# A transformer trunk on one core: one modulation row summed on VectorE in place of TensorE

## The chip, the cores and the metric

The kernel runs on one core of a Trainium2 chip. The time is the device time of one execution in microseconds (us), and the median of several runs is given. The core has five engines that run side by side: TensorE (PE in the profile; its weight loads are PEld), VectorE (DVE), ScalarE (ACT), GpSimd (POOL) and SyncE (SP), which here only issues DMA transfers. Engines wait for each other through semaphores, and each runs its own list of instructions in order.

## The reference, cut to what matters

There are two decoder layers over 512 tokens of width 1024, with 16 heads of 64. Each layer derives six rows of 1024 numbers (shift, scale and gate, once for attention and once for the feed-forward part) from the conditioning vector `c`:

```python
c_act = jax.nn.silu(c)
for i in range(DEPTH):
    mod = jnp.einsum('bd,dm->bm', c_act, w_mod[i]) + b_mod[i]
    sh_a, sc_a, gt_a, sh_f, sc_f, gt_f = jnp.split(mod, N_MOD, axis=-1)
    h = modulate(rmsnorm(x, g_mix_pre[i]), sh_a, sc_a)
    ...                                   # q, k, v; stick-breaking attention in layer 0
    x = x + gt_a[:, None, :] * rmsnorm(o, g_mix_post[i])
    h = modulate(rmsnorm(x, g_ffn_pre[i]), sh_f, sc_f)
    ...                                   # gated feed-forward part with a causal convolution of 3 taps
    x = x + gt_f[:, None, :] * rmsnorm(y, g_ffn_post[i])
```

`modulate(h, shift, scale)` is `h * (1 + scale) + shift`. One such row is a product of a vector of 1024 with a matrix of 1024 x 1024: 4 MB of weights are read once for few operations each. In layer 0 the attention weight of a key is its own sigmoid times the product of (1 - sigmoid) over the keys between it and the query.

## The kernel before, in words

**Staging.** A first stage (`begin`, to about 56 us) makes the shift and scale of layer 0's attention, the modulated input, and the first projections. Then `attention` runs layer 0's heads to about 220 us; the output projection, the feed-forward part and layer 1 follow.

**The loop over heads.** `attention` goes through h = 0 to 16, of which the last only finishes head 15. For each head it writes four blocks of scores, of 512, 384, 256 and 128 keys (`scores`: two matmuls into a PSUM bank `ps`). Of each block ScalarE makes two sigmoids (`bt` in SBUF, and `ps` in place), VectorE scans the second into running products (`om` for 512 and 384 keys, in place in `ps` for the short ones), and GpSimd (long blocks) or VectorE (short ones) multiplies `bt` by it (`stick`). The blocks of the head before are transposed (`pa` to `at`), and after each second head `weighted` multiplies them with the values into a bank `po`. All banks come from one pool of eight in turn, so a matmul into a new bank waits until the bank's last reader is done. TensorE's time between is filled with the projections of later heads (`pqk`, from weight tiles `wf` that ScalarE and GpSimd split into high and low parts `wh` and `wl`; three matmuls make one product), in portions that the table `UNITS` sets. `queries` and `keys` take a finished projection apart into `qa`, `qb`, `kh` and `kl`.

**Modulation rows beside the heads.** The three rows that layer 0 needs after its attention are made in steps, by generators in a `Background`, between the heads:

- `mod_part_pe` (lines 175 to 200) makes a row's columns on TensorE: for each half of 512 columns four loads of 512 KB (`wm`), then a group of 16 matmuls into a bank `pm` (line 191), a transpose of it on VectorE (`mf`, 194), and small copies and one reduction into the columns `mc`. It does the scale and the shift of the feed-forward part, SC_F and then SH_F: four groups.
- `mod_row` (202 to 230) sums the gate row GT_A on VectorE: for each of eight blocks of 128 rows two loads of 256 KB and two multiply-adds of 128x512 (`acc`, 223); then two transposes (`tr`), two reductions, and small steps; the gate line is written to memory (`gtd`) and broadcast back (`gb`), and multiplied by a gain into `gt` (249).

Each head's end steps the first background from head 1 and the second from head 2 on; odd heads step the first once more, ahead of `weighted`.

**What sets the order.** TensorE and SyncE run in the order in which the program is written; ScalarE, VectorE and GpSimd are ordered by a scheduler.

Of the kernel before, what the change touches and what calls it, by code (L numbers as in the profile page):

```python
# [8 lines left out]
F32 = mybir.dt.float32  # L9
# [6 lines left out]
P = 128  # L16
# [21 lines left out]
def trunk(ctx, tc, x, c, w_mod, b_mod, g_mix_pre, g_mix_post, w_qkv, w_o, w_fg, b_fg,  # L38
# [8 lines left out]
    def nm(s):  # L47
        serial[0] += 1
        return f"{s}_{serial[0]}"
# [4 lines left out]
    def slot(s, dt=F32R):  # L54
        return sb.tile([P, 512], dt, tag="slot", name=nm(s), bufs=NS)
# [17 lines left out]
    make_identity(nc, idn)  # L73
    onesf = cst.tile([P, P], F32, name="onesf")
    nc.vector.memset(onesf, 1.0)
    ones = cst.tile([P, P], F32R, name="ones")
    nc.vector.tensor_copy(ones, onesf)
    mhalf = cst.tile([P, 1], F32, name="mhalf")
    nc.vector.memset(mhalf, -0.5)
    mask = cst.tile([P, P], F32, name="mask")  # L80
# [16 lines left out]
    def b_col(l, comp):  # L97
        return colA[:, 48 * l + 8 * comp : 48 * l + 8 * comp + 8]

    def g_col(l, comp):  # L100
        o = (96 if comp == SC_A else 112) + 8 * l
        return colA[:, o : o + 8]
# [40 lines left out]
    def mod_part(l, comp):  # L143
        row = comp in (GT_A, GT_F)
        acc = sb.tile([P, D], F32, tag="acc", name=nm("acc"), bufs=1)
        lo_c = comp * D
        if row:
            nc.gpsimd.memset(acc, 0.0)
            nc.sync.dma_start(acc[0:1, :], b_mod[l : l + 1, lo_c : lo_c + D])
        for d in range(ND):  # L150
            w = t4("wm")
            nc.sync.dma_start(w, w_mod[l, d * P : (d + 1) * P, lo_c : lo_c + D])
            if d == 0 and not row:
                nc.vector.tensor_scalar(acc, w, csil[:, 0:1], None, op0=ALU.mult)
            else:
                nc.vector.scalar_tensor_tensor(acc, w, csil[:, d : d + 1], acc, op0=ALU.mult, op1=ALU.add)  # L156
            yield
        turned, part = t4("tr"), sb.tile([P, 32], F32, tag="part", name=nm("part"), bufs=1)
        nc.vector.transpose(turned, acc)
        nc.vector.tensor_reduce(part, turned.rearrange("p (b c) -> p b c", c=32), axis=AX.X, op=ALU.add)  # L160
        yield
        s = quadrants(part, 32, nc.gpsimd)
        if row:
            gp = t4("gp")
            yield from mod_line(l, comp, s, [gp[:, :512], gp[:, 512:]])
            return
        res = cst.tile([P, ND], F32, name=nm("mc"))
        columns_of(res, s, nc.gpsimd)
        yield
        nc.vector.tensor_tensor(res, res, b_col(l, comp), op=ALU.add)  # L170
        if comp in (SC_A, SC_F):
            nc.vector.scalar_tensor_tensor(res, res, 1.0, g_col(l, comp), op0=ALU.add, op1=ALU.mult)
        made[l, comp] = res

    def mod_part_pe(l, comp):

        res = cst.tile([P, ND], F32, name=nm("mc"))
        for h in range(2):
            c0 = comp * D + 512 * h
            w = []  # L180
            for i in range(4):
                if i == 2:
                    yield
                w.append(t4("wm") if i % 2 else sb.tile([P, D], F32, tag="xn", name=nm("wm"), bufs=2))
                nc.sync.dma_start(w[i].rearrange("p (d e) -> p d e", d=2),
                                  w_mod[l].rearrange("(d p) e -> p d e", p=P)[:, 2 * i : 2 * i + 2, c0 : c0 + 512])
            yield
            ps = bank("pm")
            for d in range(ND):
                q = 32 * (d % 4)  # L190
                nc.tensor.matmul(ps[q : q + 32, :], c32[:, d, :], w[d // 2][:, 512 * (d % 2) : 512 * (d % 2) + 512],
                                 start=d < 4, stop=d > 3, tile_position=(0, q))
            f = slot("mf", F32)
            nc.vector.transpose(f, ps)
            columns_of(res[:, 4 * h : 4 * h + 4], quadrants(f[:, ::32], 16, nc.vector), nc.vector)
            yield
        nc.vector.tensor_tensor(res, res, b_col(l, comp), op=ALU.add)
        if comp in (SC_A, SC_F):
            nc.vector.scalar_tensor_tensor(res, res, 1.0, g_col(l, comp), op0=ALU.add, op1=ALU.mult)
        made[l, comp] = res  # L200

    def mod_row(l, comp):

        lo_c = comp * D
        acc, part = [slot("acc", F32) for _ in range(2)], sb.tile([P, 32], F32, tag="part", name=nm("part"), bufs=1)

        def load(d):
            r = [slot("wm", F32) for _ in range(2)]
            for h in range(2):
                nc.sync.dma_start(r[h], w_mod[l, d * P : (d + 1) * P, lo_c + 512 * h : lo_c + 512 * h + 512])  # L210
            return r

        for h in range(2):
            nc.gpsimd.memset(acc[h], 0.0)
            nc.sync.dma_start(acc[h][0:1, :], b_mod[l : l + 1, lo_c + 512 * h : lo_c + 512 * h + 512])
        w = load(0)
        for d in range(ND):
            yield
            now = w
            if d < ND - 1:  # L220
                w = load(d + 1)
            for h in range(2):
                nc.vector.scalar_tensor_tensor(acc[h], now[h], csil[:, d : d + 1], acc[h], op0=ALU.mult, op1=ALU.add)
        yield
        for h in range(2):
            turned = slot("tr", F32)
            nc.vector.transpose(turned, acc[h])
            nc.vector.tensor_reduce(part[:, 16 * h : 16 * h + 16], turned.rearrange("p (b c) -> p b c", c=32), axis=AX.X, op=ALU.add)
        yield
        yield from mod_line(l, comp, quadrants(part, 32, nc.vector), [slot("gp", F32) for _ in range(2)])  # L230

    def mod_line(l, comp, s, gp):

        g = (g_mix_post if comp == GT_A else g_ffn_post)[l].rearrange("(o n) -> o n", o=1)
        for h in range(2):
            nc.sync.dma_start(gp[h], g[:, 512 * h : 512 * h + 512].to_broadcast([P, 512]))
        rows = sb.tile([32, 32], F32, tag="gtr", name=nm("gtr"), bufs=1)
        nc.vector.transpose(rows, s)
        yield True
        line = dr.tile([1, D], F32, name=nm("gtd"))  # L240
        nc.sync.dma_start(line.rearrange("o (b r) -> (o b) r", r=32), rows)
        yield True
        wide = t4("gb")
        nc.sync.dma_start(wide, line.to_broadcast([P, D]))
        yield True
        res = sb.tile([P, D], F32, tag="gt", name=nm("gt"), bufs=2)
        for h in range(2):
            cs = slice(512 * h, 512 * h + 512)
            nc.vector.tensor_tensor(res[:, cs], wide[:, cs], gp[h], op=ALU.mult)
        made[l, comp] = res  # L250
# [346 lines left out]
    def attention(l, qk, vt, ot, filler, units, bgs):  # L597


        get = cums_of.get(l)  # L600
        late, ats, cums = None, {}, {}
        for h in range(NH + 1):
            p, hd = divmod(h, 2)
            done = [0, 0]

            def fill(n=1):
                done[0] += n
                u = (units[h] * min(done[0], 12) + 11) // 12 - done[1]
                done[1] += u
                filler.run(u)  # L610

            if h < NH and hd == 0:
                ot.append((slot("oh"), slot("ol")))
            if get and h < NH:
                for i in range(h, min(h + 2, NH)):
                    if i not in cums:
                        cums[i] = get(i)
            probs = {}
            for qb in range(NT - 1, -1, -1):
                if h < NH:  # L620
                    ps, n = scores(l, hd, qb, qk[p, 0], qk[p, 1])
                    probs[qb] = stick(ps, n) if l % 2 == 0 else fox(ps, qb, cums[h])
                    fill(2)
                if late and qb == 2:
                    ats[late[1] % 2] = transposed(late[0])
            fill(2 if h < NH else 10)
            if h % 2:
                for bg in bgs[:1]:
                    bg.step()
            if late and hd == 0:  # L630
                weighted(p - 1, vt, ats, ot[p - 1])
                ats = {}
            fill(12)
            late = (probs, h)
            if h:
                for bg in bgs[: 1 + (h > 1)]:
                    bg.step()
# [196 lines left out]

    cums_of = {}
    for l in range(DEPTH):
        bgs = [Background([(l, SC_F), (l, SH_F)], mod_part_pe), Background([(l, GT_A)], mod_row)] if l == 0 else []
        scale = -0.125 if l % 2 else 0.125
        vt, qk, kl[:] = {}, {}, low_rooms()
        if l == 0:  # L840
# [173 lines left out]
```

## Time and profile before

| | |
|---|---|
| median of three runs | 1255.88 us (1254.57 to 1257.66) |
| the profiled execution | 1257.99 us, its span in the trace 1256.2 us |
| mean granted TensorE clock | 0.996 |
| busy: TensorE, VectorE, ScalarE, GpSimd | 98%, 56%, 47%, 23% of the span |

Times in the rows of the prediction are microseconds from the start of that span. "x16" behind a row means 16 instructions shown as one, and what stands in square brackets is how long the engine had been idle ahead of it, and for whom.

### The profile page before, as it was taken

The numbers are of one execution on the slowest core, as the hardware profiler recorded it, in microseconds if no ns is written. First come the engines' busy times: TensorE is split into PE (matmuls) and PEld (weight loads), VectorE is DVE, ScalarE is ACT, GpSimd is POOL, SyncE is SP. The second block draws the span as 40 slices with busy tenths as digits, with TensorE's granted clock in tenths as the row PEclk, the third lists the DMA queues.
The fourth block names the chain that finished last, engine by engine and source line by source line (L and its number), as shares of the span: only waits on it lengthen the run. The fifth ranks groups of instructions, "written<-read, shape, count | busy, mean of one in ns | idle before, by whom it ended". The sixth has DMA issues, their size and how long they took to land.

```text
span 1256.2 us, 16873 instructions
## 1 busy us (share of the span) xinstructions
PE 1234.3 (98%) x6300; PEld 1024.5 (82%) x6300; DVE 707.3 (56%) x1168; ACT 587.0 (47%) x1104; POOL 286.6 (23%) x348
## 2 busy tenths in 40 slices
PE   7999999999999999999999999999999999999997
PEld 5877877789888888888887888877988888888886
DVE  5667676277788988422364665564684444442233
ACT  7576666475333333222366565665733333331221
POOL 4775555510000000000216554452000000000000
PEclk9999999999999999999999999999999999999999
DMA  9737532225586677323405433333173333333231
GB/s 286 222 123 254 181 115 94 92 68 168 168 267 232 207 248 230 102 90 99 136 1 170 125 94 118 110 113 113 38 232 117 101 93 92 100 101 98 89 99 67
DMA packets 179400, 171.29 MB, mean 136 GB/s; under 512 B 7385, under 2 KB 152177, under 8 KB 179318
## 3 DMA queue, kind: packets, MB, share of 16 engines
q1 hardware_dynamic: 179142, 170.15, 43.6%
q8 instruction: 49, 0.80, 0.3%
q14 instruction: 33, 0.27, 0.1%
q10 hardware_dynamic: 176, 0.07, 0.0%
HBM read 168.01 MB, written 2.18 MB: 135 GB/s over the span
## 4 chain that ended last, share of the span: by engine, by line
PE 88%; DVE 4%; ACT 3%; issue 2%; DMA 1%; POOL 1%; SPq 0%; ACTq 0%; POOLq 0%; DVEq 0%
PE pgu L345 13%; PE pgu L346 13%; PE pgu L344 13%; PE pd L345 6%; PE pd L344 6%; PE pd L346 6%; PE pqk L344 4%; PE pqk L346 4%; PE pqk L345 4%; PE ps L466 3%; PE po L516 3%; PE pv L344 3%; PE pv L346 3%; PE pv L345 3%; PE pa L504 3%
## 5 line engine op out<-in xcount | busy, mean ns | idle before, releaser
L270 ACT CAST wh<-wf 128x1024 fp32r<-128x1024 f32 (+2 forms) x178 | 185.4, 1042 | 288.4 <-PE pgu L345 134.5
L345 PE MATMUL pgu<-htl,wh 128*128 128x512 f32 (+1 forms) x736 | 276.3, 375 | 0.6 <-DVE htl L406 0.6
L344 PE MATMUL pgu<-hth,wh 128*128 128x512 f32 (+1 forms) x736 | 276.4, 375 | 0.0
L346 PE MATMUL pgu<-hth,wl 128*128 128x512 f32 (+1 forms) x736 | 276.1, 375 | 0.0
L271 DVE TENSOR_TENSOR wl<-wf,wh 128x1024 fp32r<-128x1024 f32 x122 | 149.3, 1224 | 215.2 <-ACT wh L270 212.8
L345 PEld LDWEIGHTS pgu<-htl,wh 128*128 128x128 f32 x736 | 138.5, 188 | 26.1 <-DVE htl L406 1.0
L344 PEld LDWEIGHTS pgu<-hth,wh 128*128 128x128 f32 x736 | 138.5, 188 | 25.1
L346 PEld LDWEIGHTS pgu<-hth,wl 128*128 128x128 f32 x736 | 138.5, 188 | 24.6
L271 POOL TENSOR_TENSOR wl<-wf,wh 128x1024 fp32r<-128x1024 f32 (+3 forms) x56 | 129.8, 2321 | 108.6 <-ACT wh L270 106.4
L344 PE MATMUL pd<-wh,yh 128*128 128x512 f32 x288 | 112.0, 389 | 0.0
L345 PE MATMUL pd<-wl,yh 128*128 128x512 f32 x288 | 112.0, 389 | 0.0
L346 PE MATMUL pd<-wh,yl 128*128 128x512 f32 x288 | 112.0, 389 | 0.0
L357 POOL TENSOR_TENSOR r<-v,mhalf 128x1 f32<-128x1 f32 x32 | 17.6, 551 | 404.6 <-DVE v L353 404.6
L344 PE MATMUL pqk<-hth,wh 128*128 128x512 f32 (+1 forms) x240 | 94.1, 392 | 0.0
L346 PE MATMUL pqk<-hth,wl 128*128 128x512 f32 (+1 forms) x240 | 92.2, 384 | 0.4 <-POOL wl L271 0.4
L345 PE MATMUL pqk<-htl,wh 128*128 128x512 f32 (+1 forms) x240 | 92.1, 384 | 0.0
L926 ACT ACTIVATE cv<-cv 128x512 f32<-128x512 f32 x44 | 27.9, 633 | 133.8 <-DVE cv L925 133.8
L156 DVE SCALAR_TENSOR_TENSOR acc<-wm,csil,acc 128x1024 f32<-128x1024 f32 x52 | 66.7, 1282 | 10.9 <-DMA wm<-in_w_mod_dram 10.3
L344 PE MATMUL pv<-wh,hth 128*128 128x256 f32 (+1 forms) x224 | 68.8, 307 | 0.9 <-ACT hth L711 0.9
L346 PE MATMUL pv<-wh,htl 128*128 128x256 f32 (+1 forms) x224 | 67.3, 300 | 0.0
L345 PE MATMUL pv<-wl,hth 128*128 128x256 f32 (+1 forms) x224 | 67.2, 300 | 0.0
L344 PEld LDWEIGHTS pd<-wh,yh 128*128 128x128 f32 x288 | 54.1, 188 | 11.3
(202 smaller groups left out, 2221.8 us busy)
## 6 DMA issues: line engine op xcount, KB each, us to landing
wm<-in_w_mod_dram SPq DMA_DIRECT2D x72, 512.0 KB, 5.8
wf<-in_w_ffn_gate_dram SPq DMA_DIRECT2D x44, 512.0 KB, 3.9
wf<-in_w_ffn_up_dram SPq DMA_DIRECT2D x44, 512.0 KB, 4.0
wf<-in_w_ffn_down_dram SPq DMA_DIRECT2D x44, 512.0 KB, 3.5
wf<-in_w_qkv_dram SPq DMA_DIRECT2D x41, 512.0 KB, 4.0
wm<-in_w_mod_dram SPq DMA_DIRECT2D x48, 256.0 KB, 3.5
wf<-in_w_o_dram SPq DMA_DIRECT2D x16, 512.0 KB, 3.6
cum<-cumd SPq DMA_DIRECT2D x16, 512.0 KB, 4.7
```

The source lines that it names most:

```text
L156: nc.vector.scalar_tensor_tensor(acc, w, csil[:, d : d + 1], acc, op0=ALU.mult, op1=ALU.add)
L270: nc.scalar.copy(hi, src)
L271: (engine or nc.vector).tensor_tensor(lo, src, hi.bitcast(F32), op=ALU.subtract)
L344: nc.tensor.matmul(ps, ah, bh, start=first, stop=False)
L345: nc.tensor.matmul(ps, ah, bl, start=False, stop=False)
L346: nc.tensor.matmul(ps, al, bh, start=False, stop=last)
L357: nc.gpsimd.tensor_tensor(r, v, mhalf, op=ALU.pow)
L466: nc.tensor.matmul(ps[:, :n], q[hd][:, qs], k[hd][i][:, :n], start=i == 0, stop=i == 1)
L504: nc.tensor.transpose(ps[:, c : c + P], probs[qb][:, kb * P : (kb + 1) * P], idn)
L516: nc.tensor.matmul(po[HD * hd : HD * hd + HD, kb * P :], vt[p // 4, kb][:, e : e + HD], at[hd][kb], start=kb == 0, stop=kb == NT - 1, tile ...
L926: nc.scalar.activation(a, a, AF.Silu)
```

## The change

The scale row SC_F is taken from `mod_part_pe` and summed on VectorE by the same generator as the gate row, which is now `mod_vector`; for the scale it takes no bias row by DMA, and ends in columns (`columns_of`, `finish_columns`). The gate row comes first, the scale row behind it. The background on VectorE is stepped at both places of a head (two steps from head 2 on), the one on TensorE, now only with SH_F, once a head from head 1 on. An unused tile `ones` goes.

```diff
-    ones = cst.tile([P, P], F32R, name="ones")
-    nc.vector.tensor_copy(ones, onesf)
...
-    def mod_row(l, comp):
+    def mod_vector(l, comp):
-        lo_c = comp * D
+        lo_c, row = comp * D, comp == GT_A
...
         for h in range(2):
             nc.gpsimd.memset(acc[h], 0.0)
-            nc.sync.dma_start(acc[h][0:1, :], b_mod[l : l + 1, lo_c + 512 * h : lo_c + 512 * h + 512])
+            if row:
+                nc.sync.dma_start(acc[h][0:1, :], b_mod[l : l + 1, lo_c + 512 * h : lo_c + 512 * h + 512])
...
         yield
-        yield from mod_line(l, comp, quadrants(part, 32, nc.vector), [slot("gp", F32) for _ in range(2)])
+        s = quadrants(part, 32, nc.vector)
+        if row:
+            yield from mod_line(l, comp, s, [slot("gp", F32) for _ in range(2)])
+            return
+        res = cst.tile([P, ND], F32, name=nm("mc"))
+        columns_of(res, s, nc.vector)
+        finish_columns(l, comp, res)
...
             fill(2 if h < NH else 10)
-            if h % 2:
-                for bg in bgs[:1]:
-                    bg.step()
+            for bg in bgs[1:]:
+                bg.step(h > 1)
...
-        bgs = [Background([(l, SC_F), (l, SH_F)], mod_part_pe), Background([(l, GT_A)], mod_row)] if l == 0 else []
+        bgs = [Background([(l, SH_F)], mod_part_pe), Background([(l, GT_A), (l, SC_F)], mod_vector)] if l == 0 else []
```

`finish_columns` is the code that stood at the end of `mod_part` and `mod_part_pe` (add the bias column; for a scale add 1 and multiply by the gain). The number of TensorE's matmul groups `pm` goes from four to two.

SyncE's order at the end of head 3, before (`wm` of 128x2x512 are loads of `mod_part_pe`, of 128x512 those of the row on VectorE; `wf` of 128x8x128 is a projection's weights):

```order
L210 DMA wm_1096<-in_w_mod_dram 128x512
L210 DMA wm_1097<-in_w_mod_dram 128x512
L276 DMA wf_1135<-in_w_qkv_dram 128x8x128
L185 DMA wm_1200<-in_w_mod_dram 128x2x512
L185 DMA wm_1202<-in_w_mod_dram 128x2x512
```

The same place after:

```order
L208 DMA wm_1054<-in_w_mod_dram 128x512
L208 DMA wm_1055<-in_w_mod_dram 128x512
L180 DMA wm_1072<-in_w_mod_dram 128x2x512
L180 DMA wm_1074<-in_w_mod_dram 128x2x512
L208 DMA wm_1076<-in_w_mod_dram 128x512
L208 DMA wm_1077<-in_w_mod_dram 128x512
L281 DMA wf_1117<-in_w_qkv_dram 128x8x128
```

The projection's weights now stand behind four more loads.

VectorE's order from the last short blocks of head 3 to the first block of head 4 (`om` of 128x512), before:

```order
L477 SCALAR_TENSOR_TENSOR ps_1164<-ps_1164,zid 128x256
L477 SCALAR_TENSOR_TENSOR ps_1179<-ps_1179,zid 128x128
L478 TENSOR_TENSOR bt_1167<-bt_1167,ps_1164 128x255
L478 TENSOR_TENSOR bt_1182<-bt_1182,ps_1179 128x127
L477 SCALAR_TENSOR_TENSOR om_1223<-ps_1219,zid 128x512
```

And after (the scan of line 477 is line 482 there):

```order
L482 SCALAR_TENSOR_TENSOR ps_1146<-ps_1146,zid 128x256
L482 SCALAR_TENSOR_TENSOR ps_1161<-ps_1161,zid 128x128
L483 TENSOR_TENSOR bt_1149<-bt_1149,ps_1146 128x255
L483 TENSOR_TENSOR bt_1164<-bt_1164,ps_1161 128x127
L222 SCALAR_TENSOR_TENSOR acc_1047<-wm_1182,csil,acc_1047 128x512
L222 SCALAR_TENSOR_TENSOR acc_1048<-wm_1183,csil,acc_1048 128x512
L189 STREAM_TRANSPOSE mf_1200<-pm_1191 128x512
L132 COPY quad_1202<-mf_1200 32x16 x4
L133 TENSOR_REDUCE qsum_1203<-quad_1202 32x16
L139 COPY mc_939<-qsum_1203 32x4 x4
L482 SCALAR_TENSOR_TENSOR om_1225<-ps_1221,zid 128x512
```

Two multiply-adds and one group's chain now stand between the short blocks of head 3 and the first scan of head 4.

VectorE's order at the first block of head 8, before:

```order
L477 SCALAR_TENSOR_TENSOR om_1799<-ps_1795,zid 128x512
L223 SCALAR_TENSOR_TENSOR acc_1089<-wm_1787,csil,acc_1089 128x512
L439 SCALAR_TENSOR_TENSOR qa_1805<-pqk_1717,qa_1805 64x512
L439 SCALAR_TENSOR_TENSOR qb_1806<-pqk_1717,qb_1806 64x512
L477 SCALAR_TENSOR_TENSOR om_1828<-ps_1824,zid 128x384
```

And after:

```order
L482 SCALAR_TENSOR_TENSOR om_1792<-ps_1788,zid 128x512
L254 TENSOR_TENSOR gt_1913<-gb_1882,gp_1774 128x512
L444 SCALAR_TENSOR_TENSOR qa_1798<-pqk_1708,qa_1798 64x512
L444 SCALAR_TENSOR_TENSOR qb_1799<-pqk_1708,qb_1799 64x512
L482 SCALAR_TENSOR_TENSOR om_1821<-ps_1817,zid 128x384
```

The gate line's product, which takes what the broadcast `gb` brings, stands ahead of `qa` and `qb` here.

More of the change, by code (lines that the diff above doesn't have):

```diff
@@ L169, in mod_part @@
         yield
[L170 to L173, printed above, removed]
+        finish_columns(l, comp, res)
     def mod_part_pe(l, comp):
@@ L196, in mod_part_pe, with finish_columns @@
             yield
+        finish_columns(l, comp, res)
+    def finish_columns(l, comp, res):
         nc.vector.tensor_tensor(res, res, b_col(l, comp), op=ALU.add)
@@ L229, in mod_row @@
         yield
-        yield from mod_line(l, comp, quadrants(part, 32, nc.vector), [slot("gp", F32) for _ in range(2)])
+        s = quadrants(part, 32, nc.vector)
[4 more added lines that the diff above has]
+        columns_of(res, s, nc.vector)
+        finish_columns(l, comp, res)
     def mod_line(l, comp, s, gp):
```

## The prediction

> **What bounds the kernel now.** I read the page first: busy time by engine, and the chain that ended last.
>
> ```profile
> PE 1234.3 (98%) x6300; PEld 1024.5 (82%) x6300; DVE 707.3 (56%) x1168; ACT 587.0 (47%) x1104; POOL 286.6 (23%) x348
> PE 88%; DVE 4%; ACT 3%; issue 2%; DMA 1%; POOL 1%; SPq 0%; ACTq 0%; POOLq 0%; DVEq 0%
> ```
>
> TensorE is busy for 98% of the span and carries 88% of the chain. The change lies in the attention of layer 0, about 56 to 220 us, so the next view is the list of TensorE's waits in 56:300 (in total, times, longest, us), and after it that stage's windows (start:end, length, then busy us of PE, PEld, DVE, ACT, POOL with their counts, clock, DMA share, GB/s).
>
> ```profile
> PE ps L466 <- POOL kh L457: 2.0, 1, 2.0
> PE ps L466 <- DVE om L477: 0.3, 1, 0.3
> ```
>
> ```profile
> 94.00:142.00 48.00, 48.00 (x310) 37.01 (x303) 32.04 (x65) 28.45 (x61) 23.47 (x32) 1.00 0.63 207
> ```
>
> TensorE waits twice in this attention, 2.3 us in all, and runs its instructions in program order: a microsecond of its own work taken out passes to the end of the kernel, unless it then waits for what it did not wait for before. VectorE has 48.00 − 32.04 = 16 us idle in these 48. So the sum has two terms: TensorE's saving, and new waits where VectorE or a transfer comes late.
>
> **The change part by part.** *TensorE loses two of its four modulation groups `pm`.* What a group costs is not its busy time (matmuls overlap) but how far it pushes the next projection matmul:
>
> ```profile
> 92.79 0.39 PE L346 MATMUL pqk<-hth,wl 128*128 128x512 f32 x1
> 93.11 1.92 PE L191 MATMUL pm<-wm,c 128*32 128x512 f32 x16
> 94.96 0.50 PE L466 MATMUL ps<-kh,qb 128*128 128x512 f32 x1
> 95.30 0.40 PE L466 MATMUL ps<-kl,qb 128*128 128x512 f32 x1
> 95.53 0.39 PE L344 MATMUL pqk<-hth,wh 128*128 128x512 f32 x1
> ...
> 116.50 0.39 PE L346 MATMUL pqk<-hth,wl 128*128 128x512 f32 x1
> ...
> 119.24 0.39 PE L344 MATMUL pqk<-hth,wh 128*128 128x512 f32 x1
> ```
>
> From the last projection matmul ahead of the group to the first behind it pass 95.53 − 92.79 = 2.74 us, and 119.24 − 116.50 = 2.74 at the second. Between them also stand two score matmuls; three matmuls at the spacing 95.53 − 95.30 = 0.23 make 0.69. A group costs 2.74 − 0.69 = 2.05 us, two cost **4.1 us**. They are gone.
>
> *VectorE takes the scale row.* Groups by tile (min/median/max ns), and the small steps:
>
> ```profile
> L223 DVE SCALAR_TENSOR_TENSOR acc<-wm,csil,acc x16: 725/728/1585, 98.8 to 177.6; 128x512 f32<-128x512 f32 x16
> L194 DVE STREAM_TRANSPOSE mf<-pm x4: 717/717/718, 95.2 to 165.0; 128x512 f32<-128x512 f32 x4
> L227 DVE STREAM_TRANSPOSE tr<-acc x2: 669/678/687, 190.1 to 190.7; 128x512 f32<-128x512 f32 x2
> ...
> 95.95 0.69 DVE L134 COPY quad<-mf 32x16 f32<-32x16 f32 x4
> 96.68 0.25 DVE L135 TENSOR_REDUCE qsum<-quad 32x16 f32<-32x64 f32 x1
> 96.96 0.68 DVE L141 COPY mc<-qsum 32x4 f32<-32x4 f32 x4
> ```
>
> Added: 16 sums of 0.73 (11.7 us), two transposes of 0.68, two reductions of about the same (1.4), one set of quadrants and columns (some 1.7): 16 us. Removed: two chains of mf, quad, qsum and mc, 0.72 + 0.69 + 0.25 + 0.68 = 2.34 each, 4.7 us. Net some 11 us over heads 2 to 14, that is some 0.9 a head of about 11.5 us, against 16 idle in four heads. On average this is hidden; it costs where it falls ahead of a scan `om` whose PSUM bank TensorE wants back. There are two such places.
>
> *Place 1, the end of head 3.* Behind the change SyncE issues, ahead of the next weight tile `wf`, two 256-KB loads, two of 512 KB and two more of 256 KB; before, two of 256 KB.
>
> ```profile
> 94.00:96.00 2.00, 2.00 (x17) 0.99 (x10) 0.77 (x2) 0.21 (x1) 0.00 (x0) 1.00 0.80 270
> 96.00:98.00 2.00, 2.00 (x11) 1.70 (x10) 1.82 (x10) 1.46 (x3) 0.00 (x0) 1.00 1.01 288
> 98.00:100.00 2.00, 2.00 (x17) 1.82 (x16) 2.00 (x3) 1.92 (x5) 0.95 (x1) 1.00 1.03 368
> 100.00:102.00 2.00, 2.00 (x12) 1.69 (x11) 1.97 (x4) 2.00 (x5) 2.00 (x5) 1.00 1.01 364
> ...
> 92.34 0.83 SPq L210 DMA_DIRECT2D wm<-in_w_mod_dram  x2
> ...
> 94.20 2.29 SPq L185 DMA_DIRECT2D wm<-in_w_mod_dram  x4
> ...
> 100.61 1.06 ACT L270 CAST wh<-wf 128x1024 fp32r<-128x1024 f32 x1
> 102.26 0.57 ACT L476 ACTIVATE ps<-ps 128x256 f32<-128x256 f32 x2
> ...
> 97.67 1.22 DVE L477 TENSOR_TENSOR_SCAN om<-ps,zid 128x512 f32<-128x512 f32 x1
> 102.70 1.01 DVE L477 TENSOR_TENSOR_SCAN ps<-ps,zid 128x256 f32<-128x256 f32 x2 [0.25 <-ACT ps L476]
> 103.62 0.60 DVE L478 TENSOR_TENSOR bt<-bt,ps 128x255 f32<-128x255 f32 x2
> ...
> 110.58 0.22 PE L466 MATMUL ps<-kh,qa 128*128 128x128 f32 x1
> ```
>
> With `wf`'s own 0.52 MB that is 2.62 MB from 92.3 on. At the windows' 270, 288, 368 and 364 GB/s the DMA engines, which are full there (share 1.0), have moved 2.58 MB of it by 102.0: I take 102.2 for its landing, with 99 (if the loads overlap better) and 103.5 as ends. ScalarE comes to the split of `wf` in its turn and waits for it; the same turn ended at 102.26 + 0.57 = 102.83, 2.22 us behind the split's start at 100.61. So it now ends at 104.4. VectorE then does the two scans (1.01), two products (0.60), two sums (1.46), the chain of 2.34 and the scan of head 4's first block (1.22): 104.4 + 6.6 = 111.0, with small gaps 111.4. The matmul at 110.58 takes the bank which that scan frees, and it stands where it stood, since one group is gone ahead of it and one is added. **Wait: 0.8 us**, ends 0 (landing under 101.3) and 2.1 (landing at 103.5).
>
> *Place 2, heads 7 and 8.* Here before's third group stands; behind the change the second stands there, and the gate row ends here as well, so that VectorE has the copy `ol`, the mf chain, and the gate row's two transposes and reductions ahead of head 7's first scan. Then the gate line goes to memory and back.
>
> ```profile
> 139.56 1.92 PE L191 MATMUL pm<-wm,c 128*32 128x512 f32 x16
> ...
> 147.87 0.22 PE L466 MATMUL ps<-kh,qb 128*128 128x128 f32 x1
> 159.45 2.37 PE L516 MATMUL po<-at,v 128*64 128x512 f32 x16
> ...
> 153.47 1.22 DVE L477 TENSOR_TENSOR_SCAN om<-ps,zid 128x512 f32<-128x512 f32 x1 [2.34 <-ACT ps L476]
> ...
> 335.66 0.57 SPq L244 DMA_DIRECT2D gb<-gtd  x1
> ...
> 341.50 0.69 DVE L249 TENSOR_TENSOR gt<-gb,gp 128x512 f32<-128x512 f32 x1 [0.19 <-DMA gb<-gtd]
> ```
>
> With one group gone everything on TensorE comes 2.05 earlier: the group ends at 139.56 + 1.92 − 2.05 = 139.4. Behind it 0.7 (`ol`) + 2.34 + 2.7 + 1.22 (the scan) make 7.0, of which `ol` mostly lies beside the group: the scan ends at 145.7 to 146.4, nearer the first. The matmul of 147.87, due at 145.8, wants the scan's bank. Wait 0 to 0.6, I take 0.15. The broadcast `gb` took 341.50 − 335.66 = 5.8 us in the other layer; issued at about 150 it is there at 155.5, and `gt` blocks VectorE from the end of head 8's scan (153.47 + 1.22 − 2.05 = 152.6) until then. `gt` (0.7), `qa` and `qb` behind it end at 157.5; the matmul at 159.45, due at 157.4, wants their bank. Wait 0 to 1.2, I take 0.4.
>
> *The rest costs nothing.* The removed copy at the start and the small fills have nobody waiting. The scale row's loads and its last steps fall in heads 9 to 14, spread out as the gate row's were before, and there the sums that stood in those heads are replaced one for one or nearly. The wait of 2.0 us for `kh` at the last pair has the same queue ahead of it as before and only shifts.
>
> *Sum:* −4.1 + 0.8 + 0.15 + 0.4 = −2.75 us. The profiled execution took 1257.99 us, so 1255.2 beside it; that run stands 2.1 above the median of 1255.88, so the median comes to **1253.1**.
>
> One rule of the Trainium skill bears on the size of a wait. "TensorE: Matmul & The Clock Gate" (Part 1: The HAM clock gate) warns of gaps on TensorE above about 3 us, behind which the clock is halved. Here a shorter gap was enough:
>
> ```profile
> 218.45 0.50 PE L466 MATMUL ps<-kh,qa 128*128 128x512 f32 x1 [2.04 <-POOL kh L457]
> 219.34 0.63 PE L345 MATMUL po<-wl,oh 128*128 128x512 f32 x1
> ```
>
> By the page a wait of 2 us would cost 2; by this row the matmuls behind such a gap take 0.63 in place of 0.39, for about 3.4 us, some 1.5 us more. The waits in my sum are under 1 us and stay clear of it; at the upper end of place 1 (2.1 us) it would apply.
>
> **The rivals.**
> (a) *All 4.1 us, no new wait.* Speaks for it: 16 us idle on VectorE, and the wait of place 1 is gone if `wf` lands a microsecond sooner. Against: the DMA engines are full from 96 to 102. 1255.88 − 4.1 = 1251.8.
> (b) *Slower: VectorE's sums and GpSimd's products hold each other up.* GpSimd multiplies two blocks a head just when the sums run:
>
> ```profile
> L478 POOL TENSOR_TENSOR bt<-bt,om x32: 856/1096/1517, 71.3 to 232.2; 128x511 f32<-128x511 f32 x16, 128x383 f32<-128x383 f32 x16
> 177.00 2.23 DVE L223 SCALAR_TENSOR_TENSOR acc<-wm,csil,acc 128x512 f32<-128x512 f32 x2
> ```
>
> One sum of 16 took 1.585 in place of 0.728 us, beside a long product. If with four sums a head each of them took that, a head would have 4 × 0.86 = 3.4 us more on VectorE; the idle time left is some 16/4 − 0.9 = 3.1 a head, much of it not at the right moment, so I put the wait at 1 us in each of eight heads: −4.1 + 8 + 0.55 + 0.8 = +5.2, 1261. It decides once about two of four sums are stretched. One in 16 speaks against it. The Trainium skill says of the two engines, in "SBUF — State Buffer" (SBUF: two separate sides), that such operations take an exclusive lock, the loser blocked throughout; the trace bears out one clear case.
> (c) *The saving is swallowed further on*, at the keys of the last pair or at the gate line: the wait of 2.0 us there would have to grow by what is saved. Its producers wait for TensorE's own results and so come earlier with it. Time as before, 1255.9.
>
> **How the numbers follow.** Forecast (net −1.5 to −3.5 us) 0.59, (a) 0.25, (b) 0.06, (c) 0.10. About 0.3%, 3.8 us, is what a measurement of this kernel can tell from no change: faster is under 1252.1, slower over 1259.7. Faster gets most of (a) and a little of the forecast, 0.26; slower most of (b), 0.06; the rest, 0.68, is within. The range reaches below (a) by the scatter of the runs, 1250.8, and above to (c) with both waits at their upper ends and the slow clock behind one, −4.1 + 2.1 + 0.6 + 1.2 + 1.5 = +1.3, so 1257.2, with scatter 1257.6.
>
> **What would show it right or wrong.** TensorE's waits: a new row of 0.5 to 1 us for `om` near 110, one under 0.5 near 146, one for `qa`/`qb` near 157; instructions of `pm` halved to 32; the stage's end, the wait for `kh` at 216.0, moved to about 213.3. `wh` on ScalarE near 102 with a wait for a DMA shows place 1. Sums: 32 rows with a mean under 0.8; a mean above 1.1 is (b). I am wrong if TensorE's waits sum to over 3 us in the stage, or if the stage ends earlier and a later one gives it back.

## The result, and the profile after

The changed kernel takes 1265.69 us against 1257.06 us of the kernel before (medians of six runs each): the ratio is 1.0068, with a 95% interval of 1.005 to 1.0087. It is slower by 0.7%, 8.6 us, where 1253.1 was forecast, and it lies outside the range. The profiled execution took 1263.67 us, 2.0 below its median.

The page after, the busy times and the chain that ended last by engine:

```profile
PE 1230.7 (98%) x6268; PEld 1021.9 (81%) x6268; DVE 723.8 (57%) x1176; ACT 586.7 (46%) x1104; POOL 287.1 (23%) x350
PE 85%; DVE 6%; ACT 3%; DMA 3%; issue 2%; POOL 1%; SPq 0%; ACTq 0%; DVEq 0%; POOLq 0%
```

TensorE has 32 matmul rows fewer, as announced, and VectorE 16.5 us more. Three per cent of the chain have gone from TensorE to VectorE and DMA. TensorE's waits in 56:300 (in total, times, longest, us) had two rows in the attention before; now:

```profile
PE ps L471 <- DVE om L482: 5.1, 3, 3.1
PE ps L471 <- POOL kh L462: 2.0, 1, 2.0
PE pm L186 <- DVE om L482: 0.9, 1, 0.9
PE po L349 <- DVE om L482: 0.9, 1, 0.9
PE pt L402 <- DVE xn L392: 0.8, 1, 0.8
PE ps L471 <- DVE mc L195: 0.8, 1, 0.8
PE po L521 <- DVE qb L444: 0.8, 1, 0.8
```

Where they stand, from TensorE's timeline after (start, us, engine, line, operation; in brackets the idle time ahead of it and its releaser):

```profile
102.38 1.92 PE L186 MATMUL pm<-wm,c 128*32 128x512 f32 x16 [0.90 <-DVE om L482]
111.96 0.33 PE L471 MATMUL ps<-kh,qa 128*128 128x128 f32 x1 [1.79 <-DVE om L482]
150.51 0.33 PE L471 MATMUL ps<-kh,qb 128*128 128x128 f32 x1 [3.06 <-DVE om L482]
163.06 1.40 PE L521 MATMUL po<-at,v 128*64 128x512 f32 x6 [0.75 <-DVE qb L444]
226.15 0.33 PE L471 MATMUL ps<-kh,qa 128*128 128x128 f32 x1 [0.77 <-DVE mc L195]
228.22 0.50 PE L349 MATMUL po<-wh,oh 128*128 128x512 f32 x1 [0.88 <-DVE om L482]
```

These six are new: 0.90 + 1.79 + 3.06 + 0.75 + 0.77 + 0.88 = 8.15 us, twice what the two groups gave back. Laid beside the trace of before, matmul by matmul, the changed kernel runs 1.6 us ahead at 57 us and 3.7 us behind at 235. Most of the lead is not the change's: in the trace of before the granted clock was 0.52 from 21.0 to 24.5 us, in the one after 1.00, and about 1.0 of the 1.6 us arises there. So the attention of layer 0 lost some 5.35 us: −4.1 + 8.15, and about 0.2 more at each gap. Another 1.6 us is lost by 290, most of it in the wait for `xn`, told of at the end, and 0.3 behind that. From 57 us on that makes 7.3 us; the two profiled executions show no more of the 8.6 us between the medians.

**Place 2, the wait of 3.06 us.** VectorE and GpSimd at this place before:

```profile
143.34 0.68 DVE L141 COPY mc<-qsum 32x4 f32<-32x4 f32 x4
145.36 2.80 POOL L478 TENSOR_TENSOR bt<-bt,om 128x511 f32<-128x511 f32 x2 [11.74 <-DVE om L477]
148.19 4.75 POOL L271 TENSOR_TENSOR wl<-wf,wh 128x1024 fp32r<-128x1024 f32 x2
```

VectorE after, ahead of the scan that TensorE waits for, and GpSimd beside it:

```profile
143.73 0.69 DVE L226 STREAM_TRANSPOSE tr<-acc 128x512 f32<-128x512 f32 x1
144.36 4.25 DVE L139 COPY mc<-qsum 32x4 f32<-32x4 f32 x4
148.64 0.69 DVE L227 TENSOR_REDUCE part<-tr 128x16 f32<-128x512 f32 x1
149.24 1.21 DVE L482 TENSOR_TENSOR_SCAN om<-ps,zid 128x512 f32<-128x512 f32 x1
...
143.43 2.40 POOL L276 TENSOR_TENSOR wl<-wf,wh 128x1024 fp32r<-128x1024 f32 x1 [8.09 <-ACT wh L275]
145.84 2.39 POOL L276 TENSOR_TENSOR wl<-wf,wh 128x1024 fp32r<-128x1024 f32 x1
```

Four copies of 32x4 numbers, 0.68 us in the trace of before, took 4.25. They ended at 148.61; less the last two, of 0.16 each, that is 148.3, where GpSimd's second weight split ended (145.84 + 2.39 = 148.23). A transpose (0.69) and a small reduction (0.25) beside the first split took what they took before. The two splits are the same ones: before, they stood behind the two products `bt` of this head, and the copies were done 4 us ahead of them; after, the scheduler had put them ahead of these products, and the copies met them. The copies' group after (min/median/max ns; before, the longest of 16 took 164):

```profile
L139 DVE COPY mc<-qsum x12: 158/160/2329, 110.0 to 224.7; 32x4 f32<-32x4 f32 x8, 32x8 f32<-32x8 f32 x4
```

**Place 1, the waits of 0.90 and 1.79 us.** VectorE, ScalarE and SyncE after:

```profile
100.70 0.75 DVE L222 SCALAR_TENSOR_TENSOR acc<-wm,csil,acc 128x512 f32<-128x512 f32 x1 [4.19 <-DMA wm<-in_w_mod_dram]
103.02 1.05 ACT L275 CAST wh<-wf 128x1024 fp32r<-128x1024 f32 x1 [6.05 <-DMA wf<-in_w_qkv_dram]
110.68 1.22 DVE L482 TENSOR_TENSOR_SCAN om<-ps,zid 128x512 f32<-128x512 f32 x1
...
90.68 0.83 SPq L208 DMA_DIRECT2D wm<-in_w_mod_dram  x2
93.57 0.86 SPq L281 DMA_DIRECT2D wf<-in_w_qkv_dram  x1
94.52 4.48 SPq L208 DMA_DIRECT2D wm<-in_w_mod_dram  x4
```

VectorE stood 4.19 us for a sum's weights, ScalarE 6.05 for `wf`. From the first load's issue to the split of `wf` pass 103.02 − 90.68 = 12.3 us; the forecast had 102.2 − 92.3 = 9.9, since it counted the 2.62 MB issued up to `wf` and not the four loads of 256 KB issued behind it. These shared the engines: from 90 to 103 us the transfers moved 3.6 MB, where the two make 3.67 MB together.

**The end, the waits of 0.77 and 0.88 us.** VectorE and GpSimd in the last heads:

```profile
221.43 2.30 DVE L132 COPY quad<-part 32x32 f32<-32x32 f32 x4
224.88 1.22 DVE L482 TENSOR_TENSOR_SCAN om<-ps,zid 128x512 f32<-128x512 f32 x1
226.02 0.14 DVE L195 TENSOR_TENSOR mc<-mc,colA 128x8 f32<-128x8 f32 x1
226.19 1.10 DVE L197 SCALAR_TENSOR_TENSOR mc<-mc,colA 128x8 f32<-128x8 f32 x1
...
220.74 2.52 POOL L276 TENSOR_TENSOR sl<-wf,sh 128x512 fp32r<-128x512 f32 x2
226.18 1.09 POOL L483 TENSOR_TENSOR bt<-bt,om 128x511 f32<-128x511 f32 x1 [2.85 <-DVE mc L195]
```

The scale row ends here, among the last heads' scans, not in heads 9 to 14, and here too small copies (2.30 for 0.7 us) and a last operation (1.10 for 0.16) are held up: they end at 223.7 and 227.3, GpSimd's operations beside them at 223.3 and 227.3.

### The profile page after: what moved, and what is told of

Same layout as the page of the kernel before. It is cut to its first block, busy times and chain, and to the rows that moved or that the text cites. A ratio compares the mean times of both kernels' runs of the same rounds, so it can differ in the third digit from the quotient of the medians.

```text
span 1261.9 us, 16846 instructions
## 1 busy us (share of the span) xinstructions
PE 1230.7 (98%) x6268; PEld 1021.9 (81%) x6268; DVE 723.8 (57%) x1176; ACT 586.7 (46%) x1104; POOL 287.1 (23%) x350
## 4 chain that ended last, share of the span: by engine, by line
PE 85%; DVE 6%; ACT 3%; DMA 3%; issue 2%; POOL 1%; SPq 0%; ACTq 0%; DVEq 0%; POOLq 0%
PE pgu L350 13%; PE pgu L351 13%; PE pgu L349 13%; PE pd L350 6%; PE pd L351 6%; PE pd L349 6%; PE pqk L349 3%; PE pqk L351 3%; PE pqk L350 3%; PE po L521 3%; PE pv L349 3%; PE ps L471 3%; PE pv L350 2%; PE pv L351 2%; PE pa L509 2%
## 5 line engine op out<-in xcount | busy, mean ns | idle before, releaser
L349 PEld LDWEIGHTS pd<-wh,yh 128*128 128x128 f32 x288 | 54.1, 188 | 11.3
```

What stands on the lines that cost most here:

```text
L349: nc.tensor.matmul(ps, ah, bh, start=first, stop=False)
```

## The experiments

**Copies as reductions.** VectorE's small copies are written as a reduction over an axis of one element; TensorE's and SyncE's orders stay as in the changed kernel.

```diff
+    def small(engine, dst, src):
+        if engine is nc.vector:
+            nc.vector.tensor_reduce(dst, src.unsqueeze(2), axis=AX.X, op=ALU.add)
+        else:
+            engine.tensor_copy(dst, src)
-            engine.tensor_copy(u[:, i * n : (i + 1) * n], src[32 * i : 32 * i + 32])
+            small(engine, u[:, i * n : (i + 1) * n], src[32 * i : 32 * i + 32])
...
```

> The changed kernel with VectorE's small SBUF-to-SBUF copies (quad and mc, of 32 partitions) written as reductions over an axis of one element; TensorE's and SyncE's order is the same. Theory 1 (blocking): at 144.4 us of the changed kernel four such copies took 4.25 us in place of 0.68, since they wait for two weight splits of GpSimd (2.4 us each) to end; a reduction does not wait for them. Then the four take 0.7 us, the wait of 3.06 us for om at 150.5 falls under 0.5, those at 226 and 228 (0.77 and 0.88) shrink, and the time falls by 4.5 to 6.5 us to 2 to 4 us above the kernel before. Rival (amount): VectorE is late because of the work added to it and waits as long with any instruction of that length: the copies' place still takes over 3 us, and the time stays within 1.5 us of the changed kernel, 7 to 9 us above the kernel before.

Measured: 1258.3 us against 1256.61, ratio 1.0014 (1.0005 to 1.0024), 1.7 us above the kernel before; most of the loss is gone. VectorE and GpSimd of this kernel at place 2:

```profile
145.05 0.60 DVE L129 TENSOR_REDUCE mc<-qsum 32x4 f32<-32x4 f32 x4
146.28 1.21 DVE L488 TENSOR_TENSOR_SCAN om<-ps,zid 128x512 f32<-128x512 f32 x1
148.15 0.80 DVE L201 TENSOR_TENSOR mc<-mc,colA 128x8 f32<-128x8 f32 x1
...
144.09 2.40 POOL L282 TENSOR_TENSOR wl<-wf,wh 128x1024 fp32r<-128x1024 f32 x1 [8.30 <-ACT wh L281]
146.51 2.41 POOL L282 TENSOR_TENSOR wl<-wf,wh 128x1024 fp32r<-128x1024 f32 x1
```

The same two splits run beside the same place, and the four take 0.60 us. The one operation there that still has two inputs in SBUF, the sum with the bias column, takes 0.80 in place of 0.17 and ends at 148.95 with the split (148.92). The amount of VectorE's work is the same as in the changed kernel, so the rival falls. The gain is above the expected range, in part because the scheduler now also puts `qa` and `qb` ahead of the gate line's product, and the wait of 0.75 us went with it. The wait of 0.90 us at place 1 is missing too, and that is not the edit's doing: the weights of the sum ahead of it were used at 99.64 us in place of 100.70, though SyncE's order is the same. The wait of 1.79 us stays, at 1.77.

**GpSimd's two splits taken away.** The copies stay copies; the low parts of two weight tiles are left out and filled with zero.

```diff
+        tiles.append(w)
+        if len(tiles) in (11, 12):
+            nc.scalar.copy(hi, w)
+            nc.gpsimd.memset(lo.bitcast(F32), 0.0)
+        else:
+            split(hi, lo, w, engine)
-        split(hi, lo, w, engine)
```

> The changed kernel with GpSimd's two weight splits at 143.4 and 145.8 us replaced by fills with zero (the low parts of these two weight tiles are left out); VectorE's copies stay copies, and all other orders are the same. If it is GpSimd's two-input work that holds VectorE's copies up, the four mc copies at 144.4 take 0.7 to 1 us in place of 4.25, the wait of 3.06 us for om falls under 0.7, and the time falls by 3 to 4.5 us to 4 to 6 us above the kernel before. If a copy on VectorE is slow there for a reason of its own (its 32 partitions, a transfer), they still take over 3 us and nothing moves.

Measured: 1261.54 us against 1256.42, ratio 1.0043 (1.0027 to 1.0059), 5.1 above the kernel before, as expected, although the end's wait grew from 0.77 to 2.34 us (why, the next run shows) and that of 0.90 us at place 1 is missing here as well. VectorE and GpSimd of this kernel, and TensorE's wait behind them:

```profile
142.12 1.44 DVE L132 COPY quad<-mf 32x16 f32<-32x16 f32 x4
144.99 0.64 DVE L139 COPY mc<-qsum 32x4 f32<-32x4 f32 x4
...
142.06 0.95 POOL L293 MEMSET wl<- 128x1024 f32 x1 [6.93 <-PE pv L357]
143.83 0.95 POOL L293 MEMSET wl<- 128x1024 f32 x1 [0.76 <-PE pv L357]
...
147.53 0.33 PE L478 MATMUL ps<-kh,qb 128*128 128x128 f32 x1 [0.23 <-DVE om L489]
```

With nothing of GpSimd beside them the copies take 0.64 us, and the wait is 0.23 in place of 3.06. The other four, `quad`, now start inside the first fill and take 1.44 in place of 0.66, the first of them until the fill ends: a GpSimd operation that only writes holds a copy up as well. With the reductions this shows place 2 from both sides: it takes both, a copy on VectorE and work of GpSimd.

**The shift row's loads early.**

```diff
-                for bg in bgs[: 1 + (h > 1)]:
-                    bg.step()
+                for i, bg in enumerate(bgs[: 1 + (h > 1)]):
+                    bg.step(1 if i else 2 if h == 1 else h != 4)
```

> The changed kernel with the shift row's four loads of the first half issued together at the end of head 1, so that they stand ahead of the gate row's loads and the next weight tile lies behind 1 MB at the end of head 2 and not behind 2.1; its first matmul group then stands at the end of head 2, as the first group of the kernel before, its second where it stood. Theory (transfers at place 1): the waits of 0.90 us for om ahead of the group and of 1.79 us at 112 go, the one of 3.06 at 150 stays: 2.5 to 3.5 us less than the changed kernel, 5 to 6 above the kernel before. Rival (amount of VectorE's work): the waits move to another head and the time stays within 1 us.

Measured: 1261.78 us against 1256.61, ratio 1.0045 (1.003 to 1.006), 5.2 above the kernel before. TensorE's waits of this kernel:

```profile
147.49 0.33 PE L471 MATMUL ps<-kh,qb 128*128 128x128 f32 x1 [3.05 <-DVE om L482]
223.88 0.33 PE L471 MATMUL ps<-kh,qa 128*128 128x128 f32 x1 [2.34 <-DVE mc L195]
225.94 0.52 PE L349 MATMUL po<-wh,oh 128*128 128x512 f32 x1 [0.88 <-DVE om L482]
```

Nothing is left ahead of 147 us: both waits of place 1 were the transfers' (the first group moved with the loads, so that the order of the two is tried together). Their size scatters with the landing: in the three kernels of these experiments that keep SyncE's order there (the reductions, the run without the two splits, the one without the scale row's sums), `wf` was split 11.3, 11.4 and 11.8 us behind the first load's issue in place of 12.3, and the wait ahead of the group was 0, 0 and 0.27 us in place of 0.90, while that of 1.79 us stood in all three.

The end's wait grew from 0.77 to 2.34, as in the run above, but VectorE is no later there: the scan ends 6.1 us behind the matmul that had waited for `kh` in all three kernels (226.10 − 220.01, 223.82 − 217.74, 223.07 − 216.99). TensorE comes 1.6 us sooner, since the granted clock between the two was 1.00 here (218 to 222 us), and 0.71 and 0.50 in the changed kernel (220 to 224 us). The slow stretch hid 1.6 us of the wait there.

**Both edits.**

> Both edits together. If the two places are independent, as the trace of the changed kernel suggests, the gains add: 7 to 9.5 us less than the changed kernel, so from 1 us below the kernel before to 1.5 above it. If VectorE's amount of work is the cause, at most 3 us less.

Measured: 1254.68 us against 1256.61, ratio 0.9988 (0.9979 to 0.9998): 1.9 below the kernel before, a little more than expected. The gains add, and what TensorE still waits for is the end (0.77 and 0.88 us), and for `kh` and `xn`.

**The changed kernel without the scale row's sums.**

```diff
+    def mod_none(l, comp):
+        res = cst.tile([P, ND], F32, name=nm("mc"))
+        nc.vector.memset(res, 0.0)
+        finish_columns(l, comp, res)
+        yield
```

> The changed kernel without the scale row's loads and sums (its columns then hold only bias and gain): the gate row still takes two steps a head. Theory: the waits of heads 3 to 8 come of the gate row's double pace and its end, not of the scale row's sums, so that only the waits at 226 and 228 us go: 1.5 to 2.5 us less than the changed kernel, 6 to 7 above the kernel before. Rival (the scale row's 16 sums are what costs): at least 6 us less, no slower than the kernel before.

Measured: 1262.52 us against 1256.61, ratio 1.0049 (1.0034 to 1.0064), 5.9 above the kernel before and 2.7 below the changed one, a little more than the 1.5 to 2.5 expected. TensorE's waits for `om` in it:

```profile
PE ps L482 <- DVE om L493: 5.1, 3, 3.1
```

They are as long as in the changed kernel, and both waits of the end are gone. So the loss up to head 8 did not come of the sums of the scale row. What the change leaves there without them is the gate row at two steps a head and the shift row's loads and groups in earlier heads; at place 1 the run with the loads early moved the second by itself, at place 2 the two were not tried apart.

**A group's price.** The kernel before, with half of the matmuls of the scale row's groups.

```diff
-            for d in range(ND):
+            for d in range(4 if comp == SC_F else ND):
```

> The kernel before with half of the matmuls of the scale row's two groups left out (8 of 16 rows of the profile each; half of the sum is missing). It prices a group: at 2.05 us each, as the prediction took it, 2.05 us less than the kernel before, 0.2%. If TensorE's saving does not pass to the end, no change.

Measured: 1254.3 us against 1256.42, ratio 0.9987 (0.9978 to 0.9996), 2.1 less (0.5 to 2.8 by the interval). TensorE's saving passes to the end, and the size agrees with the price that the prediction read off.

**The scale row's last operations on GpSimd**, on top of both edits.

```diff
-        finish_columns(l, comp, res)
+        nc.gpsimd.tensor_tensor(res, res, b_col(l, comp), op=ALU.add)
+        nc.gpsimd.tensor_scalar(res, res, 1.0, 1.0, op0=ALU.add, op1=ALU.mult)
+        nc.gpsimd.tensor_tensor(res, res, g_col(l, comp), op=ALU.mult)
```

> Both edits (reductions, the shift row's loads early) and the last three small operations of the scale row on GpSimd, so that they no longer stand between two scans of the last head on VectorE, where they took 0.79 and 1.10 us in place of 0.14 and 0.16 beside GpSimd's product. The wait of 0.9 us for om at the output projection goes, that of 0.8 ahead of it stays: 0.8 to 1.3 us less than with both edits alone, 2.5 to 3.5 below the kernel before. If the blocking only moves to GpSimd's product of that head, no change.

Measured: 1253.19 us against 1256.42, ratio 0.9976 (0.9967 to 0.9986), 3.2 below. Both waits of the end are gone, not one of them.

**One more step of the scale row in head 10**, on top of both edits.

```diff
-                bg.step(h > 1)
+                bg.step((h > 1) + (h == 10))
```

> Both edits and one more step of the scale row in head 10, so that its end comes half a head sooner. If the end is what TensorE waits for (0.8 and 0.9 us), both waits go: 1.2 to 2 us less than with both edits alone. Rival: four sums on end in head 10 make a new wait there of the same size, no change.

Measured: 1252.01 us against 1256.42, ratio 0.9972 (0.9963 to 0.9981): 4.4 below the kernel before by medians and 3.5 by the ratio, the lowest median of all. That is 2.7 less than with both edits alone by medians, 2.0 by the ratios, where 1.2 to 2 was expected. TensorE's waits of this kernel between 56 and 300 us:

```profile
PE ps L477 <- DVE kl L469: 1.5, 1, 1.5
PE pt L408 <- DVE xn L398: 0.4, 1, 0.4
PE pgu L356 <- DVE htl L417: 0.3, 1, 0.3
PE ps L477 <- DVE om L488: 0.3, 1, 0.3
PE pgu L355 <- ACT hth L416: 0.2, 1, 0.2
```

Not one of the six is left, and in place of the old wait of 2.0 us for `kh` stands one of 1.5 for `kl`. VectorE still does all the work that the change gave it.

**The control.** The kernel before with its copies as reductions.

> The kernel before with VectorE's small copies written as reductions, its order unchanged on every engine. In its trace no such copy stood beside work of GpSimd that held it up (at most 0.17 us each), and TensorE did not wait for them: no change, within 0.1%. If reductions are simply a better form, it gains as the changed kernel did.

Measured: 1256.3 us against 1256.42, ratio 0.9998 (0.9989 to 1.0008). The form alone brings nothing here, where no such copy meets an operation of GpSimd.

**All of it together.**

> Reductions, the shift row's loads early, the extra step in head 10 and the scale row's last operations on GpSimd. With the extra step the end of the scale row no longer makes TensorE wait, so that moving its last operations adds nothing: within 0.5 us of the kernel with the extra step, 3.5 to 5 us below the kernel before.

Measured: 1252.78 us against 1256.42, ratio 0.997 (0.996 to 0.998), 0.8 above the kernel with the extra step alone by medians, outside the 0.5 expected; by the ratios, 0.997 and 0.9972, the two are the same, so nothing is gained by it. TensorE's waits shift: 0.81 us for `kh` and a new one of 0.80 for a weight split of GpSimd.

## Why the prediction was wrong, point by point

- *TensorE's saving, 4.1 us:* right. Two halves of a group were worth 2.1 us, and the best version saves 4.4 us by medians, 3.5 by the ratio.
- *Net 11 us on VectorE are hidden on average:* right, and it was not the cause. VectorE was busy for 16.5 us more in the changed kernel, the held-up time included, and for 12.2 us more in the kernel with the extra step, which hides them.
- *Place 1, 0.8 us:* the mechanism was right, the size was not. It measured 0.90 + 1.79 = 2.7. The term that failed is the landing of `wf`, which left out the loads issued behind it; and the scan that the group's own bank waits for was not looked at (0.90 in this trace, 0 to 0.27 in others).
- *Place 2, 0.15 us:* this step failed, 3.06 us in its place. The chain was summed with durations from rows in which GpSimd did nothing that holds such a copy up: 0.68 us for four copies that took 4.25. The order of GpSimd's list at this place, which the change had turned round, was not laid beside VectorE's.
- *The gate line, 0.4 us:* 0.75 was measured, within the bounds given.
- *"The rest costs nothing":* this step failed as well, by 0.77 + 0.88 us. The scale row's end was put in heads 9 to 14, and it came at 217 to 227 us, ahead of and between the last head's scans. With the clock at 1.00 behind the wait for `kh`, the first of the two is 2.34 us.
- *Rival (b)* named the right mechanism, VectorE and GpSimd holding each other up, and the right sign, but was given a chance of 0.06 and the wrong pair: the sums beside the products `bt`. Some sums were held up (2.17 and 2.47 us beside weight splits at 119.8 and 128.0 us) without a wait of TensorE, and the mean of the 32 sums, 0.92 us, lies between the two marks that had been set (0.8 and 1.1). What counted were copies of a few numbers beside the splits, up to 2.33 us each. The one sum of 1.585 us in the trace of before was a sign of it; its price was worked out as a mean per head, and should have been looked for ahead of each scan that TensorE waits for.
- The Trainium skill states in "SBUF — State Buffer" (SBUF: two separate sides) that VectorE in a two-port mode, or with two inputs in SBUF against a GpSimd operation that reads SBUF, shares a port pair with GpSimd under an exclusive lock, and that whoever comes second is blocked for the whole instruction. The traces agree: a copy's end at 148.3 with GpSimd's at 148.23, 0.80 us for a two-input sum until 148.95, and a reduction of the same data that was not blocked. In which mode a copy ran, no trace shows.
- *The sign for being wrong* came: TensorE's waits in the stage sum to over 10 us, where 3 had been set as the limit.
- *Open:* the wait for `xn` at 273 us, 0.2 to 0.9 us in every kernel with the gate row at two steps, hangs on a transfer of 512 KB that took 4.9 to 5.6 us to its first use there and 3.8 to 3.9 in the three kernels with the order of before. It is there without the scale row's loads too. The cause was not tried.

## What to carry to other kernels

Before work is moved to VectorE, lay GpSimd's order beside VectorE's at each place where the matrix engine waits for VectorE: a copy of a few numbers, or an operation with both inputs in SBUF, took as long here as the GpSimd operation that it met, and a reduction over one element did the same copy without that. The order to look at is that of the changed program, since a scheduler can turn round what stood well apart before. A transfer's landing is counted with what is issued behind it while it is under way. An average of idle time says that work fits, not that it fits ahead of the scan that is waited for. Before waits of two traces are compared, compare the granted clock ahead of them.

## What had not been expected of the hardware

- A copy of 32x4 numbers took 2.33 us beside one weight split of GpSimd, 15 times its 0.16; a fill by GpSimd, which reads nothing, made a group of four copies 0.8 us longer.
- Windows of the changed kernel behind two of TensorE's waits (start:end, length, TensorE busy, granted clock, DMA share, GB/s):

```profile
150.00:152.00 2.00, 1.49 (x7) 1.00 0.00 0
152.00:154.00 2.00, 2.00 (x10) 1.00 0.02 2
220.00:222.00 2.00, 1.99 (x7) 0.71 0.84 227
222.00:224.00 2.00, 2.00 (x8) 0.50 0.09 35
```

  The wait of 3.06 us ahead of 150.5 was followed by a granted clock of 1.00, the one of 2.03 us ahead of 220.0 by 0.71 and 0.50. The length of a gap did not decide it here. The kernel before with reductions has the same wait of 2.03 us for `kh` (ahead of 217.5), with a clock of 1.00 from 218 to 222; the wait of 3.05 us in the kernel with the loads early was followed by 0.50 from 148 to 150. So the prediction's price of 1.5 us behind a gap of 2 us holds for the execution that it was read from, and not for each.
